# The S5 layer with a plain fp32 input projection, its tap products on one engine, and its constants and Toeplitz work in other places of the order

## The chip, the cores and the metric

The kernel runs on one core of a Trainium2 chip. Its engines are TensorE (matrix products; PE for the products and PEld for the loading of weights in the profile), VectorE (DVE), ScalarE (ACT), GpSimd (POOL) and SyncE (SP). SyncE, ScalarE and GpSimd issue transfers into DMA queues. Each engine runs its own instructions in order and waits on semaphores for the others. The metric is the device time of one execution in microseconds (us), as the median of several executions.

## The reference, cut to what matters

The kernel computes one inference step of a four-layer decoder trunk for 512 prompt tokens and 8 x 8 sampled tokens, 576 columns in all, in fp32. The change is in the token mixer of the first layer, an S5 state-space layer with 64 groups of 16 channels and 64 complex states per group:

```python
u = (x @ w_in)                                    # 1024 -> 1024
dt = jnp.exp(log_dt)[:, None]
mag = jnp.exp(lam_r * dt)
lb_r, lb_i = mag * jnp.cos(lam_i * dt), mag * jnp.sin(lam_i * dt)
den = lam_r * lam_r + lam_i * lam_i
f_r = ((lb_r - 1.0) * lam_r + lb_i * lam_i) / den
f_i = (lb_i * lam_r - (lb_r - 1.0) * lam_i) / den
bb_r, bb_i = _cmul(f_r[..., None], f_i[..., None], b_re, b_im)
bu = einsum('blgi,gpi->blgp', ug, bb)             # complex inputs of the states
h = associative_scan(h[t] = lb * h[t-1] + bu[t])  # complex states, all t
y = einsum(h_r, c_re) - einsum(h_i, c_im) + d_skip * u
g = gelu(y);  out = (g * sigmoid(g @ w_glu + b_glu)) @ w_out
```

Three more token mixers and, after each mixer, an expert channel mixer follow; the change does not touch them.

## The kernel before, in words

**The algorithm.** Time is cut into chunks of 8 steps: 64 chunks of the prompt and 8 sampled sequences, so `NC` = 72 columns. Within a chunk the layer is a Toeplitz product (tiles `T0` to `T2`, each for 16 of the 64 groups); between chunks a recurrence carries the state (tile `HS`), and a last product takes the states into the outputs. All of it stands in `s5` (from L263).

**Projection.** The input x comes in eight tiles `xraw` of 128x576. Each is split into a high and a low part of a reduced fp32 type (`x0H` by ScalarE, L130; `x0L` by VectorE, L131), and each weight block `wr` of 128x1024 into `wh` (ScalarE, L69) and `wl` (VectorE, L79). u comes in eight blocks m of 128 rows; a block takes 8 steps k, two halves of 288 columns and three products each (high by high, high by low, low by high), 384 products in all, issued in `mm` (L126). ScalarE copies a block out (L435) and writes it to the DRAM tile `du` (L436, ScalarE's queue). After every fourth block SyncE loads the four blocks back in another order into `U8` (eight transfers, L442, `U` in the rows).

**Parameters.** `params()` (L317 to L411) is a generator: the projection loop takes steps of it in between, so its small operations on VectorE stand between the splits. It works out exp, sine and cosine (128x64 tiles), the powers 0 to 8 of the step factor (`PW`, L295 to L300 through `cmul`), and the input matrix `bb`, `b2` (twelve operations of 128x512, L380 to L385). GpSimd negates halves of `c1` and `b2` (L353, L354) and makes twelve of sixteen groups of output taps `CL` (three operations of 128x576 each, `powered`, L311 to L315, called at L360). VectorE makes the eight back steps (`BL`, `tb`, six 128x512 operations each, L401), which TensorE transposes and ScalarE copies into `BT` (`turn`, L388 to L394), and then the last four groups of taps (L409).

**Order after the projection.** SyncE loads the initial state into `HS` (L450) and the skip vector `dk` (L453); GpSimd multiplies it by a diagonal into `dm` (L454) and then sets the three T tiles to zero (L458). TensorE multiplies `BT` by `U` (L488); VectorE copies the results to `HS` (L490) and ScalarE to `SS` (L491). GpSimd works out the chunk powers `AP` (L500 to L508), 24 operations in three rounds after six that set up the first power. `toeplitz(q)` (L460 to L480), for q = 0 to 3, copies `bb` on ScalarE into `BR`, multiplies it by `CL` on TensorE, copies the product to `KT`, adds `dm` on GpSimd (L476) and places the result in T with sixteen transfers, eight each from SyncE and GpSimd. `toeplitz(0)` and `toeplitz(1)` are issued ahead of the recurrence, 2 and 3 after it, followed by the products of T with `U` (L579) and their copies to `U` (L582).

**Recurrence.** `steps` (L520 to L533) makes two products and two sums on VectorE per job. The first phase goes over seven positions of the chunks (128x512 operations), the second over seven chunk blocks (128x64), the third over the seven positions again (128x448), and a last step gives the final states `HF`, with a copy (L567). `swap` (L510 to L518) puts a slice of `HS` into `H2` (`H` in the rows): two copies on ScalarE and two transfers from SyncE. One swap is issued before the recurrence; the other eight are gathered in a list and issued at L574, behind the transfers of all four `toeplitz` calls. Then the output products with `CL` and `H2` run (from L585); VectorE adds them to `U` (L596), and SyncE and GpSimd write the result to DRAM. GELU, the gate and the output projection end the layer.

`Weights` (L48) loads raw blocks ahead (three buffers), splits them, and hands them out with `next`; `next_raw` hands out a raw block.

Of the kernel before, what the change touches and what calls it, by code (L numbers as in the profile page):

```python
# [19 lines left out]
KD = 8  # L20
# [27 lines left out]
class Weights:  # L48
# [71 lines left out]
class K:  # L120
# [142 lines left out]
    def s5(self):  # L263
        tc, nc, I, O = self.tc, self.nc, self.I, self.O
        V, G, A, S = nc.vector, nc.gpsimd, nc.scalar, nc.sync
        R0, R1, R2, R3, R4, LB, L0, L1 = (ExitStack() for _ in range(8))
        p0 = self.pool(R0, "s5a")
        p1 = self.pool(R1, "s5b")
        p2 = self.pool(R2, "s5c")
# [4 lines left out]
        b1, b2, c1, c2 = (p2.tile([128, 64, 16], F32, name=k) for k in ("b1", "b2", "c1", "c2"))  # L274
        xH = p2.tile([128, KD, NT], F32R, name="x0H"); xL = p2.tile([128, KD, NT], F32R, name="x0L")
        xraw = {}

        def xload(k):
            xraw[k] = p2.tile([128, NT], F32, name="xraw", bufs=XB)
            S.dma_start(xraw[k], I["xT0"][:, k, :])  # L280
# [3 lines left out]
        for k in range(1, XB):  # L284
            xload(k)
        PW = p0.tile([128, 9, 2, 64], F32, name="PW")
# [4 lines left out]
        tg = p2.tile([128, 4, 9, 16], F32, name="tg")  # L291
# [10 lines left out]
        def powered(E, jobs, a, b, last):  # L302
# [7 lines left out]
            for o, t, pw, ab in todo:  # L310
                E.tensor_tensor(o, pw[0], ab[0], op=OP.mult)  # L311
            for o, t, pw, ab in todo:
                E.tensor_tensor(t, pw[1], ab[1], op=OP.mult)
            for o, t, pw, ab in todo:
                E.tensor_tensor(o, o, t, op=last)  # L315

        def params():  # L317
# [5 lines left out]
            for i, _ in enumerate(self.exp_(dt, ldt, p2, "e")):  # L323
# [4 lines left out]
                if i % 4 == 3:  # L328
                    yield
# [3 lines left out]
            for i, _ in enumerate(self.sincos(sn, cs, ang, p2)):  # L333
                next(ex, None)
                if i % 3 == 2:
                    yield
# [6 lines left out]
            yield  # L343
            tmp = p2.tile([128, 4, 8, 16], F32, name="BL", bufs=4).rearrange("p a b c -> p a (b c)")[:, :, :64]
            for b in (1, 2, 4):
# [4 lines left out]
                yield  # L350
# [5 lines left out]
            def taps(E, e0, t):  # L356
                e = slice(e0, e0 + 4)
                powered(E, [(CL[:, e], t, e, slice(0, 9))], c1, c2, OP.subtract)

            for e0 in range(0, 4 * NG, 4):  # L360
                taps(G, e0, tg)
# [12 lines left out]
            yield  # L374

            for h in range(2):
# [9 lines left out]
                yield  # L386

            def turn(q, BL):  # L388
                for i in range(2):
                    o = self.psB()  # L390
                    for a in range(4):
                        nc.tensor.transpose(o[:, 128 * a:128 * a + 128], BL[i][:, a].rearrange("p s j -> p (s j)"), self.ident)
                    e = 8 * q + 4 * i
                    A.activation(BT[:, e:e + 4, :].rearrange("p a b -> p (a b)"), o, AF.Copy)  # L394


            last = None
            for q in range(8):
                BL, tb = ([p2.tile([128, 4, n, 16], F32, name=k, bufs=m)[:, :, :8] for _ in range(2)] for k, n, m in (("BL", 8, 4), ("tb", 9, 2)))
                e = [slice(8 * q + 4 * i, 8 * q + 4 * i + 4) for i in range(2)]  # L400
                powered(V, [(BL[i], tb[i], e[i], slice(7, None, -1)) for i in range(2)], bb, b2, OP.subtract)  # L401
                yield
                if last:
                    turn(*last)
                last = (q, BL)
                yield
            turn(*last)
            for e0 in range(4 * NG, 64, 4):
                taps(V, e0, p2.tile([128, 4, 9, 16], F32, name="tb", bufs=2))  # L409
                yield  # L410


        par = params()
        for k in range(KD):
            self.split(xH[:, k, :], xL[:, k, :], xraw[k])
            if k + XB < KD:
                xload(k + XB)
            if k == 1:
                self.W.load(2)
            if k == 4:  # L420
                for t, n in ((b1, "b1"), (b2, "b2"), (c1, "c1"), (c2, "c2")):
                    S.dma_start(t, I[n])
            if k == 0:
                self.W.split(1)
            next(par)
        du = self.dram.tile([D, NT], F32, name="du")
        duv = du.rearrange("(g j) (s c) -> s j g c", j=16, s=8)
        for m in range(KD):
            w = self.W.next()
            o = [self.ps(), self.ps()]  # L430
            self.proj([(o[q][:, :288], slice(288 * q, 288 * q + 288)) for q in range(2)], w, xH, xL)
            self.W.ahead()
            uT = p2.tile([128, NT], F32, name="xraw", bufs=XB)
# [3 lines left out]
            for _ in range(3):  # L437
                next(par, None)
# [4 lines left out]
        for _ in par:  # L443
            pass
        R2.close()
        p2 = self.pool(R2, "s5d")
# [5 lines left out]
        dk = p2.tile([128, 32], F32, name="dk"); dm = p2.tile([128, 32, 16], F32, name="dm")  # L452
        S.dma_start(dk, I["s5_d"])  # L453
# [1164 lines left out]
```

## Time and profile before

| what | us |
|---|---|
| median of three executions | 3258.47 (3254.98 to 3260.18) |
| profiled execution, its own time | 3255.29 |
| its span, first to last instruction | 3253.5 |
| TensorE busy (PE) | 2994.6 (92%) |
| VectorE busy (DVE) | 2746.4 (84%) |
| GpSimd busy (POOL) | 1363.6 (42%) |
| ScalarE busy (ACT) | 1157.5 (36%) |

The mean granted clock of TensorE is 0.964 of full speed. Times within the profile count from the first instruction. The busy shares are averages over all four layers; the S5 layer is the first, and its first output product starts at 208.48 us. A row of the chain of waits gives start, duration and what was being waited for or done. A row of the timeline gives start, busy time, engine, line, operation, out<-in by tile names, shape, and in brackets the idle time before it with what ended it; several like operations in a row stand as one with their count (x8), and what such a row then gives is their time together. A row by stretches gives the stretch, its length, the busy us of PE, PEld, DVE, ACT and POOL with their instructions, the granted clock, the mean share of the DMA engines in use, and GB/s. "SPq" and "ACTq" are the issue of transfers by SyncE and ScalarE. The busy times of two operations of one engine that follow each other can overlap by 0.05 to 0.1 us, since an operation starts before the one ahead of it is out.

### The profile page before, as it was taken

The page shows a single profiled execution, that of the slowest core. Times are in us where ns is not written, and L with a number is a line of the kernel's source. Part 1 is how long each engine was busy: PE and PEld are TensorE (multiplying, and loading weights), DVE is VectorE, ACT ScalarE, POOL GpSimd, SP SyncE. Part 2 cuts the span into 40 slices and gives each one's busy share as a digit, 9 for nine tenths or more (in the row PEclk, how much of TensorE's full clock was granted, in tenths as well). Part 3 has the DMA queues.
Part 4 walks back from the last instruction along what each step waited for, and adds up shares of the span by engine and source line. Part 5 has one row for each costly group of instructions (what it writes and reads, how often), then busy time and mean ns, then how long its engine had stood idle before and what let it go on. Part 6 is the DMA issues. An engine that isn't in the chain of part 4 may idle for free.

```text
span 3253.5 us, 45493 instructions
## 1 busy us (share of the span) xinstructions
PE 2994.6 (92%) x16316; PEld 2561.6 (79%) x16316; DVE 2746.4 (84%) x5864; ACT 1157.5 (36%) x1704; POOL 1363.6 (42%) x994
## 2 busy tenths in 40 slices
PE   5559979899999999999998897989899999999997
PEld 4558877566899888888988797656688988888986
DVE  9846798999888888888887679899888888888888
ACT  2234232256333333333333333235533333333332
POOL 7441221444354555554430022245345555555442
PEclk8879989999999999999999998989999999999998
DMA  4364324999999999999972211689899999999995
GB/s 129 61 117 145 127 111 139 328 359 340 315 343 344 334 340 337 340 340 338 342 283 94 75 57 56 223 297 387 303 331 338 340 347 335 336 332 348 353 338 201
DMA packets 332273, 862.44 MB, mean 265 GB/s; under 512 B 56199, under 2 KB 145255, under 8 KB 329334
## 3 DMA queue, kind: packets, MB, share of 16 engines
q1 hardware_dynamic: 204830, 434.41, 38.9%
q0 software_dynamic: 112960, 405.36, 34.4%
q10 hardware_dynamic: 14256, 19.77, 1.7%
q8 instruction: 128, 2.10, 0.3%
q14 instruction: 99, 0.81, 0.1%
HBM read 791.76 MB, written 71.96 MB: 265 GB/s over the span
## 4 chain that ended last, share of the span: by engine, by line
PE 70%; DVE 19%; DMA 4%; issue 2%; ACT 2%; POOL 2%; SPq 1%; DVEq 0%; ACTq 0%; POOLq 0%
PE pa L126 41%; PE pb L126 29%; DMA grow<-in_peer_u,gidx 1%; DVE prod L1486 1%; DVE grow L1525 1%; DVE ti L1339 1%; DVE sc L1335 1%; DVE ti L1333 1%; DMA x<-SD 1%; DVE tv L1331 1%; DVE tv L1337 1%; DMA wr<-in_U 1%; DVE rs L783 1%; SPq L480 1%; DVE st L767 0%
## 5 line engine op out<-in xcount | busy, mean ns | idle before, releaser
L1520 POOL DMA_INDIRECT grow<-in_peer_u,gidx x384 | 611.2, 1592 | 516.6 <-DVE acc L1533 312.2
L1520 POOL DMA_INDIRECT grow<-in_peer_v,gidx x384 | 503.0, 1310 | 720.4 <-DVE grow L1525 561.5
L131 DVE TENSOR_TENSOR vl<-vr,vh 128x1024 fp32r<-128x1024 f32 x256 | 313.8, 1226 | 251.8 <-ACT vh L130 251.2
L126 PE MATMUL pa<-vh,wwh 128*128 128x512 f32 x1536 | 478.9, 393 | 24.9 <-ACT wwh L1217 24.7
L1533 DVE SCALAR_TENSOR_TENSOR acc<-grow,gact,acc 128x1024 f32<-128x1024 f32 x380 | 485.6, 1278 | 3.5 <-DMA grow<-in_peer_v,gidx 2.5
L1525 DVE SCALAR_TENSOR_TENSOR grow<-grow,x 128x1024 f32<-128x1024 f32 x384 | 465.2, 1217 | 23.1 <-DMA grow<-in_peer_u,gidx 21.4
L126 PE MATMUL pa<-vh,wwl 128*128 128x512 f32 x1536 | 477.7, 392 | 0.0
L126 PE MATMUL pa<-vl,wwh 128*128 128x512 f32 x1536 | 477.0, 392 | 0.0
L126 PE MATMUL pb<-xH,wl 128*128 128x384 f32 x1344 | 455.0, 339 | 0.0
L126 PE MATMUL pb<-xH,wh 128*128 128x384 f32 x1344 | 454.9, 338 | 0.0
L126 PE MATMUL pb<-xL,wh 128*128 128x384 f32 x1344 | 454.3, 338 | 0.0
L130 ACT ACTIVATE vh<-vr 128x1024 fp32r<-128x1024 f32 x256 | 271.8, 1062 | 511.3 <-PE pa L126 462.8
L126 PEld LDWEIGHTS pa<-vh,wwh 128*128 128x128 f32 x1536 | 287.2, 189 | 76.5 <-ACT wwh L1217 28.7
L126 PEld LDWEIGHTS pa<-vl,wwh 128*128 128x128 f32 x1536 | 289.3, 188 | 63.6
L126 PEld LDWEIGHTS pa<-vh,wwl 128*128 128x128 f32 x1536 | 288.8, 188 | 63.8 <-DVE wwl L1219 1.8
L79 POOL TENSOR_TENSOR wl<-wr,wh 128x1024 fp32r<-128x1024 f32 x35 | 90.3, 2580 | 405.7 <-ACT wh L69 339.7
L126 PEld LDWEIGHTS pb<-xL,wh 128*128 128x128 f32 x1344 | 253.1, 188 | 7.4
L79 DVE TENSOR_TENSOR wl<-wr,wh 128x1024 fp32r<-128x1024 f32 x193 | 237.0, 1228 | 25.3 <-ACT wh L69 25.2
L126 PEld LDWEIGHTS pb<-xH,wh 128*128 128x128 f32 x1344 | 252.3, 188 | 6.5
L126 PEld LDWEIGHTS pb<-xH,wl 128*128 128x128 f32 x1344 | 252.3, 188 | 0.0
L69 ACT ACTIVATE wh<-wr 128x1024 fp32r<-128x1024 f32 x228 | 239.4, 1050 | 12.8 <-PE pa L126 10.7
L126 PE MATMUL pb<-x,wr 128*128 128x384 f32 x704 | 238.5, 492 | 0.6 <-DMA wr<-in_U 0.6
(349 smaller groups left out, 4998.3 us busy)
## 6 DMA issues: line engine op xcount, KB each, us to landing
wr<-in_U SPq DMA_DIRECT2D x256, 512.0 KB
vr<-in_peer_v SPq DMA_DIRECT2D x256, 512.0 KB
GD<-stg SPq DMA_DIRECT2D x16, 2048.0 KB
x<-GD SPq DMA_DIRECT2D x64, 512.0 KB
SD<-g ACTq DMA_DIRECT2D x88, 192.0 KB
x<-SD SPq DMA_DIRECT2D x88, 192.0 KB
wr<-in_w_q SPq DMA_DIRECT2D x32, 512.0 KB
grow<-in_peer_u,gidx POOLq DMA_INDIRECT x384
```

Of the source, the lines that this page charges most:

```text
L69: self.k.nc.scalar.activation(h[:, :nk], self.raw[self.nh], AF.Copy)
L79: e.tensor_tensor(l[:, :nk], self.raw.pop(self.ns), h[:, :nk].bitcast(F32), op=OP.subtract)
L126: self.nc.tensor.matmul(out, lhsT, rhs, start=start, stop=stop)
L130: self.nc.scalar.activation(h, src, AF.Copy)
L131: self.nc.vector.tensor_tensor(l, src, h.bitcast(F32), op=OP.subtract)
L480: (S if par else G).dma_start(Tb[q % 3][16 * s:16 * s + 16, par::2, 16 * s:], KT[r0:r0 + 16, :, :128 - 16 * s])
L783: yield V.scalar_tensor_tensor(t, y, ve, y, op0=OP.mult, op1=OP.mult)
L1331: V.max(v[:, 0:8], s)
L1333: V.max_index(i[:, 0:8], v[:, 0:8], s)
L1520: nc.gpsimd.indirect_dma_start(out=t, out_offset=None, in_=table, in_offset=bass.IndirectOffsetOnAxis(ap=gidx[:, 128 * u + j:128 * u + j + ...
L1525: V.scalar_tensor_tensor(t, t, 1.0, self.X(3 + u), op0=OP.mult, op1=OP.mult, accum_out=act[:, 128 * u + j:128 * u + j + 1])
L1533: V.scalar_tensor_tensor(acc[:, u], t, w, acc[:, u], op0=OP.mult, op1=OP.add)
```

## The change

- **Projection.** x and the weights are not split; the products are plain fp32 ones, 128 in all. The first two blocks run together over k (`next_raws`), the others one at a time (`next_raw`). All eight `xraw` tiles have their own place; `b1`, `b2`, `c1`, `c2` are loaded between the weight blocks.
- **Parameters.** `params()` runs straight through. The negations of `b2` and `c1` go to ScalarE. The chunk powers `AP` are worked out right after `PW`: eighteen operations (`cmul`) on GpSimd, the setting up and the copies on ScalarE.
- **Taps.** All sixteen groups are made by VectorE, in pairs like the back steps, after them. A back step and half a block's projection alternate.
- **Skip and zeros.** `dk` is loaded at the start on ScalarE's queue, `dm` and the zeros of `T0` and `T1` are made by GpSimd at the start. `T2` has its own place and is set to zero after the inputs.
- **Inputs.** Both evacuations of the input products are on ScalarE; the first half of the inputs runs after three quarters of the taps.
- **Reload.** Four of the eight transfers of the second reload of `U` are issued by GpSimd.
- **Toeplitz.** `dm` is added by VectorE. `toeplitz(0)` and `toeplitz(1)` are issued before the recurrence, (2) and (3) within its first phase, the products with T (`within`) beside it.
- **Swaps.** Each is issued as soon as its slice is ready in the order. The weight split of the next projection is issued after `HF`.

The diff, cut to its core:

```diff
@@ Weights
+    def next_raws(self, n):
+        self.load(n)
+        ws = [self.raw.pop(i) for i in range(n)]
+        self.nu = self.nh = self.ns = n
+        return ws
@@ s5: loads and places
-        xH = p2.tile([128, KD, NT], F32R, name="x0H"); xL = p2.tile([128, KD, NT], F32R, name="x0L")
...
+            xraw.append(p2.tile([128, NT], F32, name=f"xraw{k}"))
...
+        xload(1)
+        xload(2)
+        self.W.load(2)
+        for k in range(3, KD):
             xload(k)
+        for t, n in ((b1, "b1"), (b2, "b2")):
+            S.dma_start(t, I[n])
+        self.W.load(3)
+        for t, n in ((c1, "c1"), (c2, "c2")):
+            S.dma_start(t, I[n])
+        dk = pt.tile([128, 32], F32, name="dk"); dm = pt.tile([128, 32, 16], F32, name="dm")
+        A.dma_start(dk, I["s5_d"])
...
+        Tb = [pt.tile([128, 16, 128], F32, name=f"T{q}") for q in range(2)]
+        G.tensor_tensor(dm, self.diag[:, None, :].to_broadcast([128, 32, 16]), dk[:, :, None].to_broadcast([128, 32, 16]), op=OP.mult)
+        for t in Tb:
+            G.memset(t, 0.0)
@@ params(): runs straight, its yields are gone
-            G.tensor_scalar(c1[im], c1[im], -1.0, None, op0=OP.mult)
-            G.tensor_scalar(b2[im], b2[im], -1.0, None, op0=OP.mult)
...
-            for e0 in range(0, 4 * NG, 4):
-                taps(G, e0, tg)
+            A.activation(b2[im], b2[im], AF.Copy, scale=-1.0)
+            A.activation(c1[im], c1[im], AF.Copy, scale=-1.0)
+
+            for h in range(2):
+                rows, e = slice(64 * h, 64 * h + 64), slice(32 * h, 32 * h + 32)
+                A.activation(AP[rows, 0, 0, 0], PW[rows, 8, 0, e], AF.Copy)
+                A.activation(AP[rows, 0, 1, 1], PW[rows, 8, 1, e], AF.Copy)
+            for b in (1, 2, 4):
+                sh = [128, b, 32]
+                cmul(G, AP[:, b:2 * b, 0, 0], AP[:, b:2 * b, 1, 1], AP[:, b - 1:b, 0, 0].to_broadcast(sh), AP[:, b - 1:b, 1, 1].to_broadcast(sh),
+                     AP[:, :b, 0, 0], AP[:, :b, 1, 1], tap[:, :b, :])
@@ back(q), turn(q, BL): the eight steps as before, now functions
+        def taps(q):
+
+            for e0 in (8 * q, 32 + 8 * q):
+                es = [slice(e0 + i, e0 + i + 4) for i in (0, 4)]
+                powered([(CL[:, e], pc.tile([128, 4, 9, 16], F32, name="tb", bufs=2), e, slice(0, 9)) for e in es], c1, c2)
@@ projection
-            self.split(xH[:, k, :], xL[:, k, :], xraw[k])
...
-            self.proj([(o[q][:, :288], slice(288 * q, 288 * q + 288)) for q in range(2)], w, xH, xL)
-            self.W.ahead()
+        def uproj(ws, os, ks):
+            for k in ks:
+                for w, o in zip(ws, os):
+                    for q in range(2):
+                        self.mm(o[q][:, :288], w[:, k, :], xraw[k][:, 288 * q:288 * q + 288], k == 0, k == KD - 1)
...
-                    S.dma_start(U8[16 * s:16 * s + 16, g, :], duv[s][:, g, :])
+                    (G if m > 3 and s % 2 else S).dma_start(U8[16 * s:16 * s + 16, g, :], duv[s][:, g, :])
...
+        first = self.W.next_raws(2)
+        o = [[self.ps(), self.ps()] for _ in range(2)]
+        uproj(first, o, range(KD))
+        for m in range(2):
+            udone(m, o[m])
+        for m in range(2, KD):
+            w, o = self.W.next_raw(), [self.ps(), self.ps()]
+            for h in range(2):
+                q = 2 * (m - 4) + h
+                if q >= 0:
+                    BL = back(q)
+                uproj([w], [o], range(4 * h, 4 * h + 4))
+                if q >= 0:
+                    turn(q, BL)
+            udone(m, o)
@@ toeplitz(q), inputs, order
-            G.tensor_tensor(KT[:, :, :16], KT[:, :, :16], dm[:, 8 * q:8 * q + 8], op=OP.add)
+            V.tensor_tensor(KT[:, :, :16], KT[:, :, :16], dm[:, 8 * q:8 * q + 8], op=OP.add)
...
-            V.tensor_copy(HS[:, 9:, :, gp:gp + 2], ov[:, 8:])
+                A.activation(HS[:, 9:, :, gp:gp + 2], ov[:, 8:], AF.Copy)
...
+        for q in range(3):
+            taps(q)
+        inputs(range(0, 16, 2))
+        toeplitz(0)
+        taps(3)
+        toeplitz(1)
+        A.activation(AP[:, :, 0, 1], AP[:, :, 0, 0], AF.Copy)
+        A.activation(AP[:, :, 1, 0], AP[:, :, 1, 1], AF.Copy, scale=-1.0)
+        inputs(range(16, 32, 2))
...
+        G.memset(Tb[2], 0.0)
@@ recurrence
         for q in range(1, 8):
             steps([(H[:, :, q], H[:, :, q - 1], H[:, :, q], AP[:, 0, 0], AP[:, 0, 1])])
+            if q == 2:
+                toeplitz(2)
+                within(0)
+            if q == 5:
+                toeplitz(3)
+                within(1)
         for b in range(1, 8):
             steps([(H[:, b:b + 1, 7], H[:, b - 1:b, 7], H[:, b:b + 1, 7], AP[:, 7, 0], AP[:, 7, 1])])
-        swaps = [lambda: swap(slice(16, 73, 8))]
+        within(2)
+        within(3)
+        swap(slice(0, 9))
+        swap(slice(16, 73, 8))
         for q in range(0, 7, 2):
...
-                swaps.append(lambda i=i: swap(slice(9 + i, 73, 8)))
+                swap(slice(9 + i, 73, 8))
...
+        self.W.split(self.W.nu + 2)
```

## Rows read from the trace of the kernel before

**Rows 1.** Page, chain that ended last: share of span by engine.

```profile
PE 70%; DVE 19%; DMA 4%; issue 2%; ACT 2%; POOL 2%; SPq 1%; DVEq 0%; ACTq 0%; POOLq 0%
```

**Rows 2.** Busy us by engine (x instructions), granted clock, DMA share, GB/s, by stretch.

```profile
40.00:90.00 50.00, 19.50 (x108) 17.86 (x108) 50.00 (x30) 4.76 (x9) 49.22 (x30) 0.67 0.34 57
90.00:121.00 31.00, 27.55 (x198) 26.81 (x200) 27.73 (x42) 11.10 (x21) 0.25 (x1) 0.90 0.25 80
```

**Rows 3.** Chain that ended last, 100 to 230: start, us, what.

```profile
121.31 13.80 issue
...
136.20 5.24 POOL T L458 x3
...
143.53 0.74 POOL AP L295
...
173.15 11.23 POOL KT L476
...
206.04 2.31 DMA H<-HS
```

**Rows 4.** Timeline of VectorE (start, us, operation), 142 to 188: recurrence.

```profile
142.35 0.69 DVE L528 TENSOR_TENSOR w<-AP,HS 128x512 f32<-128x512 f32 x1 [1.78 <-POOL AP L500]
...
163.60 0.23 DVE L528 TENSOR_TENSOR w<-AP,HS 128x64 f32<-128x64 f32 x1
...
169.52 0.62 DVE L528 TENSOR_TENSOR w<-AP,HS 128x448 f32<-128x448 f32 x1
...
184.78 0.68 DVE L528 TENSOR_TENSOR w<-AP,HS 128x512 f32<-128x512 f32 x1
...
187.30 0.19 DVE L567 COPY HF<-HS 128x64 f32<-128x64 f32 x1
```

**Rows 5.** Timeline of VectorE, 38 to 119 us: the big products and taps.

```profile
38.93 1.72 DVE L380 TENSOR_TENSOR bb<-sn,b 128x512 f32<-128x512 f32 x1
...
61.41 3.50 DVE L311 TENSOR_TENSOR BL<-PW,bb 128x512 f32<-128x512 f32 x2
...
94.26 1.28 DVE L313 TENSOR_TENSOR tb<-PW,b 128x512 f32<-128x512 f32 x2
95.47 1.28 DVE L315 TENSOR_TENSOR BL<-BL,tb 128x512 f32<-128x512 f32 x2
...
118.03 0.75 DVE L311 TENSOR_TENSOR CL<-PW,c 128x576 f32<-128x576 f32 x1
```

**Rows 6.** Timeline of ScalarE and VectorE, 3 to 26: parameters.

```profile
4.00 0.68 ACT L130 ACTIVATE x0H<-xraw 128x576 fp32r<-128x576 f32 x1 [0.56 <-DMA xraw<-in_xT]
...
7.64 0.22 DVE L321 TENSOR_TENSOR den<-lr 128x64 f32<-128x64 f32 x1
...
24.47 0.22 DVE L295 TENSOR_TENSOR PW<-PW 128x64 f32<-128x64 f32 x1
```

**Rows 7.** TensorE: timeline 510 to 545 us, and chain 100 to 230 us.

```profile
515.52 29.83 PE L126 MATMUL pa<-x,wr 128*128 128x384 f32 x92
...
111.66 6.28 PE pa L126 x47
```

**Rows 8.** Timeline of SyncE, ScalarE and TensorE, 55 to 140: reloads of U.

```profile
62.11 21.82 SPq L442 DMA_DIRECT2D U<-du  x8
...
118.71 0.33 ACTq L436 DMA_DIRECT2D du<-xraw  x1
...
120.82 7.23 SPq L442 DMA_DIRECT2D U<-du  x8
...
134.53 5.58 PE L126 MATMUL pa<-U,BT 128*64 128x72 f32 x128 [5.08 <-DMA U<-du]
```

**Rows 9.** Timeline of GpSimd and ScalarE, 184 to 198: T copies, U copies.

```profile
184.67 4.17 POOL L480 DMA_DIRECT2D T<-KT  x8 [0.30 <-POOL KT L476]
188.84 0.46 POOL L476 TENSOR_TENSOR KT<-KT,dm 128x128 f32<-128x128 f32 x1
...
196.46 0.41 ACT L582 ACTIVATE U<-pa 128x288 f32<-128x288 f32 x1 [0.55 <-PE pa L126]
```

More of the change, by code (lines that the diff above doesn't have):

```diff
@@ L265, in s5 @@
         V, G, A, S = nc.vector, nc.gpsimd, nc.scalar, nc.sync
-        R0, R1, R2, R3, R4, LB, L0, L1 = (ExitStack() for _ in range(8))
+        R0, R1, R2, R4, RT, RH, LB, LC, L0, L1 = (ExitStack() for _ in range(10))
         p0 = self.pool(R0, "s5a")
         p1 = self.pool(R1, "s5b")
-        p2 = self.pool(R2, "s5c")
+        pc = LC.enter_context(tc.tile_pool(name="s5c", bufs=1, reuse_waits="tile"))
+        pt = self.pool(RT, "s5e")
+        p2 = self.pool(R2, "s5p")
         small = lambda n: p2.tile([128, 64], F32, name=n)
@@ L397, in params @@
[L397 to L414, printed above, removed]
-            self.split(xH[:, k, :], xL[:, k, :], xraw[k])
[L416 to L425, printed above, removed]
+        def back(q):
+            BL, tb = ([p.tile([128, 4, n, 16], F32, name=k, bufs=m)[:, :, :8] for _ in range(2)] for p, k, n, m in ((p2, "BL", 8, 4), (pc, "tb", 9, 2)))
+            e = [slice(8 * q + 4 * i, 8 * q + 4 * i + 4) for i in range(2)]
+            powered([(BL[i], tb[i], e[i], slice(7, None, -1)) for i in range(2)], bb, b2)
+            return BL
@@ L426, in s5 @@
+        params()
         du = self.dram.tile([D, NT], F32, name="du")
         duv = du.rearrange("(g j) (s c) -> s j g c", j=16, s=8)
-        for m in range(KD):
-            w = self.W.next()
-            o = [self.ps(), self.ps()]
-            self.proj([(o[q][:, :288], slice(288 * q, 288 * q + 288)) for q in range(2)], w, xH, xL)
-            self.W.ahead()
-            uT = p2.tile([128, NT], F32, name="xraw", bufs=XB)
+        def uproj(ws, os, ks):
[3 more added lines that the diff above has]
+                        self.mm(o[q][:, :288], w[:, k, :], xraw[k][:, 288 * q:288 * q + 288], k == 0, k == KD - 1)
@@ L434, in s5, with udone @@
+        def udone(m, o):
+            uT = p2.tile([128, NT], F32, name="uT", bufs=2)
             for q in range(2):
@@ L451, in s5 @@
         G.memset(HS[:, 8], 0.0)
[L452 to L458 removed]
         def toeplitz(q):
[L463 removed]
+            BR = p2.tile([128, 2, 8, 4, 16], F32, name="BR")
             for par in range(2):
@@ L492, in s5 @@
-        LB.close()
-        H2 = self.pool(R4, "s5h").tile([128, 73, 2, 32], F32, name="H2")
-        AP = p2.tile([128, 8, 2, 2, 32], F32, name="AP")
-        tap = p2.tile([128, 4, 32], F32, name="tap")
-        for h in range(2):
-            rows, e = slice(64 * h, 64 * h + 64), slice(32 * h, 32 * h + 32)
-            G.tensor_copy(AP[rows, 0, 0], PW[rows, 8, 0:1, e].to_broadcast([64, 2, 32]))
-            G.tensor_scalar(AP[rows, 0, 1, 0], PW[rows, 8, 1, e], -1.0, None, op0=OP.mult)
-            G.tensor_copy(AP[rows, 0, 1, 1], PW[rows, 8, 1, e])
@@ new lines, in within @@
+        def within(q):
+            for g4 in range(0, 16, 4):
+                o = self.ps()
+                for a in range(4):
+                    for h in range(2):
+                        rows = slice(64 * h, 64 * h + 64)
+                        self.mm(o[rows, NC * a:NC * a + NC], Tb[q % 3][:, g4 + a, rows], U8[:, 16 * q + g4 + a, :], True, True)
+                g = 16 * q + g4
+                A.activation(U8[:, g:g + 4, :].rearrange("p a c -> p (a c)"), o[:, :4 * NC], AF.Copy)
+        for q in range(3):
+            taps(q)
```

111 lines of the change are left out of this document (36 added, 75 removed).

## The prediction

> **What bounds the kernel now.** The whole execution is bound by TensorE: its products are most of the chain that ended last [rows 1]. That share is an average over stages, and the change edits only the first, from the start to the first output product of the state-space layer at 208.5 us. So I read the stretches of that stage next [rows 2]: VectorE is busy all of 40 to 90 us, TensorE two fifths of them; from 90 to 121 both are busy nine tenths. The chain of waits says what leads: first VectorE, then the rest of the projection on TensorE, and from 121 a chain that does not run on VectorE [rows 3]: a 13.8 us wait for the second reload of U, which also covers the wait for the skip vector; three memsets on GpSimd (5.24 us); 24 small GpSimd operations of the chunk powers, one after the other, from 143.53 (0.74 the first) to 161.6; the Toeplitz copies; a GpSimd addition that took 11.23 us; copies issued by SyncE; and the last copy into H, from 206.04 to 208.35. VectorE had finished its own last work at 187.5 [rows 4], 21 us before.
>
> The second reading is what VectorE's operations cost. Beside GpSimd's taps a pair of 128x512 products takes 3.50 us, some 1.71 each from start to start; from 92 us on, with GpSimd idle, 1.28 (94.26 to 95.47: 0.60 each), and a 128x576 tap is busy 0.75, about 0.675 from start to start as the same 0.07 overlaps [rows 5]. Each of VectorE's big operations in 40:90 thus lost 1.1 us to GpSimd's taps.
>
> By a rule of the Trainium skill ("SBUF — State Buffer", section "SBUF: two separate sides") VectorE and GpSimd share a port pair as an exclusive lock, and the loser waits a whole instruction; the trace agrees (1.71 beside, 0.60 alone).
>
> **The change, part by part.** I follow VectorE, since after the change it holds nearly all the serial work, and look for each step at what could be later than it.
>
> *Small operations.* VectorE now starts its parameters when they land; the first tile landed by 4.0 us, so 4.4. Before, den to the powers took 16.8 us (7.64 to 24.47); without seven splits of x (0.67 each from start to start), a weight split (1.14) and 0.9 us of GpSimd's interference that is 10.1. From there to the first 128x512 product (38.93) were 14.5 us; without a split (1.1) and what GpSimd stretched in seven operations (7.2 together) 6.2 [rows 5, 6]. The new GpSimd product dm gets 1 us. End: 21.7.
>
> *The big products.* 12 for bb at 0.60: 7.3. 48 for the eight back steps at 0.60: 29.0. All 48 taps at 0.675: 32.4, of which 24.3 before the first Toeplitz addition. The two additions, moved from GpSimd, 0.3 each.
>
> *Chunk powers on GpSimd,* now beside bb. Eighteen of the 24 operations stay, the other six go to ScalarE. Before, they ran beside 28 recurrence operations, which took 21.25 us (142.35 to 163.60) instead of the 17.6 of the undisturbed rate [rows 3, 4]: 3.6 us for 24. I take 4 for 18, as VectorE now has fewer gaps; the ends are 0 (all in gaps) and 13 (18 at 0.74, the whole chain). Two of the memsets (1.75 each) now lie beside two-input VectorE operations, which no row shows: 0 to 3.5; I take 0, as they kept an even 1.75 beside VectorE's copies [rows 3].
>
> Running sum: 21.7 + 7.3 + 4 + 29.0 = 62.0; with 24.3 + 0.3 + 8.1 + 0.3 the recurrence starts at 95.0.
>
> *Recurrence.* Seven steps at 2.52 per four operations, 17.6, plus 1.1 for two Toeplitz additions and a memset; the second phase 5.9 (163.60 to 169.52); the third 15.3 (169.52 to 184.78) [rows 4]: 134.9. The last swap is now issued at once, and needs what it needs now: 2.31 from its second issue to the landing [rows 3], and 0.9 for the first issue and the hand-over. First output product: **138.1** instead of 208.5, that is 70.4 earlier.
>
> *What must stay hidden for this.* (1) TensorE's projection: 128 plain products in place of 384. No row has one of 288 columns; the nearest is 92 plain products of 384 in 29.83 us, 0.324 each, by columns 0.243 for 288, against 0.134 for one of the three products replaced (47 in 6.28) [rows 7]. The bounds are 0.134 and 0.324; I take 0.243. A half block is eight products, 1.94, and eight transposes, put at 0.134 each too, 1.07: 3.0 us beside a back step of 3.6. Cover: 0.6 a step. The granted clock was 0.67 in 40:90 [rows 2]; at the lower level a half takes 6.0, but then TensorE is busy throughout, and rows 2 show the clock back at 0.90 when it was nearly so. Four buffers absorb two steps: cost 0 to 3, I take 0. (2) U's second reload: last block out at 64.7, written by 66.8 (2.1 as in 118.71 to 120.82 [rows 8]), 13.7 until the last load is used [rows 8], 80.5; ScalarE's two copies for each of eight groups 6.6 at most (0.41 each [rows 9], an estimate from a larger copy): 87.1, with 7.9 us of cover before 95.0. Four of these loads go to GpSimd's queue, behind the chunk powers there. (3) Toeplitz copies: sixteen issues each, eight on GpSimd in 4.17 [rows 9], eight on SyncE in 7.2 at most, its rate for U [rows 8]; the last begun by 110 and landed by 120, under the third phase of the recurrence. SyncE's waits stand in program order: behind the wait for the last copies stand only swaps that are due later. (4) Weight loads behind U's first reload on SyncE: due at 47, free to go at 32.
>
> *After the stage* the kernel is unchanged, and its TensorE-bound rest shifts whole: I know of no later transfer that starts at a fixed time. The two weight splits that are moved (128x1024 each, some 2.4 us together by 0.60 per 512 columns) end at about 140, before the first output product's result is due.
>
> **Sum.** The profiled execution took 3255.3 us (span 3253.5 and 1.8 around it), the median of three is 3258.5. 3255.3 - 70.4 = 3184.9 in the profile's own terms, 3188.1 against the median; I predict 3188.
>
> **Rivals.** *GpSimd starved.* The 11.23 us addition [rows 3] took 0.46 the next time [rows 9]: VectorE ran paired, gapless operations and GpSimd got in only at a gap. If the chunk powers meet this during bb, back steps and taps, which are paired likewise, they end only when VectorE itself stops for them at 95: 13 us of powers, 2.1 for four U loads, 6.9 for their landing (half of 13.7), 6.6 for the copies: 28.6 later, less the 4 of interference, 3188 + 24.6 = **3213**. Against it: in 40 to 90 us both engines took turns through the same paired operations. 20 in 100.
>
> *A reload stuck on SyncE.* Of U's first reload seven loads went within 4 us, the eighth 17 us later, after a later du write [rows 8]. The same at the second: 80.5 + 17 + 6.6 = 104.1 instead of 95: **3197**. 10 in 100.
>
> *The plain product is dearer than its row.* If one cost four of the single products (0.536), a half block would take 4.29 + 1.07 = 5.4 and TensorE would pace the eight back steps, 1.8 each beyond 3.6; the taps would end some 14 later: **3202**. The row (0.324 at 384 columns, against 0.18 for a single product of that width by the same ratio) speaks clearly against it. 3 in 100. The Trainium skill ("FP8 and Floating Point Precision", section "TensorE Precision Notes") has true fp32 as four passes, which is this case; the row disagrees, with less than two.
>
> *Slower.* If VectorE's operations do not shorten when GpSimd leaves, 108 big operations at 1.70 instead of 0.64 add 115 us: the products start at 249, **3299**. It decides from 1.29 us per operation (70.4/108 more than 0.64). The 0.60 of the stretch after 92 us speaks against it. 2 in 100. That the change does nothing (within 0.2%) gets 1.
>
> **How the numbers follow.** My forecast has 60 in 100. Its own ends: all small costs at their lower end (start, no interference) gives 130, 3180; memsets, powers at half their upper end and a TensorE lag give 151, 3201. The range of 8 in 10 takes in the stuck reload and the starved GpSimd: 3179 to 3214. The other 4 in 100 are stalls that I have not named. 0.2%, 6.5 us, is about what a measurement here can tell from no change; all cases but two lie far beyond it: faster 0.97, same 0.01, slower 0.02.
>
> **What would show it.** Right: 128x512 products at 0.6 us from 23 us on; the recurrence starting near 95 and the first output product near 138, with VectorE the chain between; the projection's products 0.24 apart. Wrong: a VectorE gap before the recurrence (U, or the powers on GpSimd); GpSimd operations of over 2 us in 22 to 95; back steps over 4 us apart (TensorE); or a stage that ends at 138 and a total that falls by much less, which would mean that the rest does not shift whole.

## The result, and the profile after

The changed kernel took 3198.91 us (median of four executions, 3194.87 to 3200.56) against 3256.72 (3253.99 to 3260.18) for the kernel before, measured again beside it: a ratio of 0.982 with a 95% interval of 0.9803 to 0.9837, 57.8 us less. The forecast was 3188, the range 3179 to 3214. The profiled execution took 3198.16 us, its span is 3195.9 and its mean granted clock 0.972.

The stage that the change edits ends 59.4 us earlier: the first output product starts at 149.05 instead of 208.48. The forecast had 138.1. So all of the gain is in the stage, and it is 11.0 us smaller than forecast. What follows the stage is as much earlier to within 2.1 us: 59.6 at 500 us, 58.6 at 1200, 57.3 at the end. These last differences are near to what kernels with the same stage show among themselves (a second profile of the changed kernel has the first output product at 149.40, and a kernel whose stage ends at 149.13 runs 1.2 us ahead of it at the end), so they are left.

The chain that ended last, on the page of after, share of the span by engine, which answers to [rows 1]:

```profile
PE 73%; DVE 18%; DMA 5%; issue 2%; ACT 1%; POOL 1%; SPq 1%; DVEq 0%; POOLq 0%; ACTq 0%
```

The stretches by engine, 40 to 90 and 5 to 80 us of after (columns as in [rows 2]):

```profile
40.00:90.00 50.00, 46.25 (x360) 37.70 (x358) 42.55 (x68) 18.37 (x48) 2.92 (x5) 1.00 0.62 109
5.00:80.00 75.00, 73.15 (x326) 57.32 (x328) 65.55 (x166) 15.82 (x36) 15.87 (x21) 1.00 0.59 162
```

In 40 to 90 us TensorE went from 19.50 us busy to 46.25, and VectorE from 50.00 to 42.55: the two have changed places, and GpSimd, busy 49.22 there before, is almost idle. From 5 to 80 us TensorE is busy 73.15 of 75. It is the engine that hardly waits (0.69 and 0.64 us, for weights), though it has fewer products to make. The clock is no cause of it: granted in full, 1.00, that is 2.4 GHz.

Now TensorE and VectorE during the back steps, from 45 to 60 us of after. First the timeline of TensorE, then that of VectorE (columns as in [rows 4]):

```profile
45.51 4.05 PE L133 MATMUL pa<-xraw,wr 128*128 128x288 f32 x16
49.39 1.04 PE L417 MATMUL pb<-ident,BL 128*128 128x128 f32 x8
50.26 4.05 PE L133 MATMUL pa<-xraw,wr 128*128 128x288 f32 x16
54.15 1.04 PE L417 MATMUL pb<-ident,BL 128*128 128x128 f32 x8
```

```profile
50.03 1.29 DVE L335 TENSOR_TENSOR BL<-PW,bb 128x512 f32<-128x512 f32 x2 [1.05 <-PE pb L417]
51.24 1.29 DVE L337 TENSOR_TENSOR tb<-PW,b 128x512 f32<-128x512 f32 x2
52.44 1.29 DVE L339 TENSOR_TENSOR BL<-BL,tb 128x512 f32<-128x512 f32 x2
54.78 1.29 DVE L335 TENSOR_TENSOR BL<-PW,bb 128x512 f32<-128x512 f32 x2 [1.05 <-PE pb L417]
```

VectorE's operations are what was forecast, a pair of 128x512 in 1.29 us and 3.6 for the six, and the taps (not shown) go at 1.34 a pair. But a step starts every 4.75 us (50.03 to 54.78) and waits 1.05 for TensorE's transposes. TensorE has no gap: half a block of the projection from 45.51 to 49.39, 3.88 us, and eight transposes to 50.26. The half block has sixteen instructions, where the forecast counted eight products. The groups by line and shape for TensorE, before and after, over the whole projection (columns: line, engine, operation, tiles, shape, count, busy us and mean ns, idle time before):

```profile
L126 PE MATMUL pa<-x0H,wh 128*128 128x288 f32 x128 | 31.2, 328 | 6.5 <-ACT wh L69 6.5
```

```profile
L133 PE MATMUL pa<-xraw,wr 128*128 128x288 f32 x256 | 67.0, 421 | 6.8 <-DMA wr<-in_w_in 6.8
```

The code makes 128 plain products (8 blocks, 8 steps k, 2 halves); the trace has 256 instructions. A plain product is two instructions of 3.88/16 = 0.2425 us, 0.485 in all. The reduced type is one instruction per product (128 of high by high for 128 in the code). At this pace the projection is 256 x 0.2425 = 62.1 us of work for TensorE (the row has 67.0 busy, as its first 144 instructions, from 5.52 to 44.63 us, were slower), where the three single products before are 384 x 0.134 = 51.5 at theirs [rows 7]: the change makes TensorE's work longer, not shorter, by 10.6 us.

The end of the stage went as forecast. The recurrence on VectorE starts at 106.05 (95.0 forecast), with no wait ahead of it; the timeline of VectorE and the chain of after (chain: start, us, what):

```profile
105.85 0.31 DVE L487 TENSOR_TENSOR KT<-KT,dm 128x128 f32<-128x128 f32 x1
106.05 0.71 DVE L552 TENSOR_TENSOR w<-AP,HS 128x512 f32<-128x512 f32 x1
```

```profile
146.54 2.32 DMA H<-HS
148.85 0.20 issue
149.05 4.50 PE pa L133 x62
```

The recurrence took 39.7 us where 39.9 was forecast (first phase 19.2 for 18.7, second 5.4 for 5.9, third 15.1 for 15.3), and from its end at 145.79 to the first product are 3.3 for 3.2; the last swap's transfer takes the 2.3 us that it took before [rows 3].

### The profile page after: what moved, and what is told of

Same layout as the page of the kernel before. It is cut to its first block, busy times and chain, and to the rows that moved or that the text cites. A ratio compares the mean times of both kernels' runs of the same rounds, so it can differ in the third digit from the quotient of the medians.

```text
span 3195.9 us, 45180 instructions
## 1 busy us (share of the span) xinstructions
PE 2993.5 (94%) x16188; PEld 2549.7 (80%) x16188; DVE 2713.2 (85%) x5872; ACT 1150.6 (36%) x1712; POOL 1270.6 (40%) x944
## 4 chain that ended last, share of the span: by engine, by line
PE 73%; DVE 18%; DMA 5%; issue 2%; ACT 1%; POOL 1%; SPq 1%; DVEq 0%; POOLq 0%; ACTq 0%
PE pa L133 42%; PE pb L133 30%; DMA grow<-in_peer_u,gidx 1%; DVE prod L1502 1%; DVE ti L1355 1%; DVE sc L1351 1%; DVE ti L1349 1%; DVE grow L1541 1%; DMA x<-SD 1%; DVE tv L1347 1%; DVE tv L1353 1%; DVE rs L799 1%; POOL grow L1536 1%; DVE prod L1520 0%; DVE st L783 0%
## 5 line engine op out<-in xcount | busy, mean ns | idle before, releaser
L79 DVE TENSOR_TENSOR wl<-wr,wh 128x1024 fp32r<-128x1024 f32 x185 | 225.5, 1219 | 23.7 <-ACT wh L69 23.6
L69 ACT ACTIVATE wh<-wr 128x1024 fp32r<-128x1024 f32 x220 | 230.9, 1050 | 11.3 <-PE pa L133 11.3
```

The costliest lines, as they stand in the source:

```text
L69: self.k.nc.scalar.activation(h[:, :nk], self.raw[self.nh], AF.Copy)
L79: e.tensor_tensor(l[:, :nk], self.raw.pop(self.ns), h[:, :nk].bitcast(F32), op=OP.subtract)
```

## The experiments

All were timed beside the kernel before; the table gives what each stage time came to. "Last projection product" is the start of its last instruction, "H" is the start of the first output product, "HS" the end of the last copy of the inputs into `HS`, which the recurrence needs. The totals of different rows differ by up to 4 us for the same stage, so the readings go by the stage times, and the totals are their control.

| kernel | last projection product | HS | recurrence | H | median us | ratio to before (95%) |
|---|---|---|---|---|---|---|
| changed kernel | 78.58 | 104.16 | 106.05 | 149.05 | 3198.91 | 0.982 (0.9803 to 0.9837) |
| the same, again | 78.96 | 105.36 | 106.45 | 149.40 | 3198.46 | 0.9825 (0.9811 to 0.9838) |
| half of the products | 65.75 | 89.70 | 97.90 | 140.87 | 3189.46 | 0.9789 (0.9773 to 0.9806) |
| taps in between | 78.60 | 106.12 | 106.16 | 149.13 | 3194.93 | 0.9803 (0.9787 to 0.9819) |
| zeros on ScalarE | 78.12 | 103.70 | 105.61 | 148.57 | 3197.96 | 0.9818 (0.9802 to 0.9835) |
| taps on GpSimd | 105.38 | 131.11 | 131.14 | 174.11 | 3222.57 | 0.9891 (0.9875 to 0.9908) |
| Toeplitz and swaps late | 79.23 | 104.91 | 106.71 | 173.91 | 3224.02 | 0.99 (0.9875 to 0.9925) |
| reload by two blocks | 87.48 | 106.42 | 114.97 | 158.02 | 3209.76 | 0.9857 (0.9833 to 0.988) |
| the same, and taps in between | 87.22 | 106.32 | 107.37 | 150.42 | 3200.22 | 0.9826 (0.9803 to 0.9848) |
| all second loads on SyncE | 78.16 | 103.51 | 105.65 | 148.73 | 3199.19 | 0.9819 (0.9796 to 0.9843) |
| both edits, loads on GpSimd | 77.94 | 95.40 | 97.99 | 141.03 | 3188.48 | 0.9799 (0.9786 to 0.9812) |
| and zeros on ScalarE | 77.62 | 95.33 | 97.67 | 140.70 | 3188.91 | 0.9799 (0.9785 to 0.9812) |

### Does TensorE pace the back steps? Half of the products left out

```diff
-                uproj([w], [o], range(4 * h, 4 * h + 4))
+                uproj([w], [o], (0, 2) if h == 0 else (5, 7))
```

> The changed kernel, with half of the projection's products left out in blocks 2 to 7 (four of the eight steps k), so that TensorE's part of a half block falls from 4.75 us (16 instructions of 0.2425 and eight transposes) to 2.8. Theory, TensorE paces the back steps: they go at VectorE's own 3.6 us each instead of 4.7, the recurrence starts at 97.4 instead of 106.05 and the first output product at 140.4 instead of 149.05; the total falls by some 8 us. Rival, the back steps wait for buffers or ScalarE's copies, whatever the products take: still 4.75 apart, 149.

Measured: H at 140.87 for 140.4 of the theory, the total 9.5 us less. The back steps follow each other at VectorE's own rate (timeline of VectorE, this kernel):

```profile
43.72 1.28 DVE L335 TENSOR_TENSOR BL<-PW,bb 128x512 f32<-128x512 f32 x2
47.33 1.28 DVE L335 TENSOR_TENSOR BL<-PW,bb 128x512 f32<-128x512 f32 x2
50.95 1.28 DVE L335 TENSOR_TENSOR BL<-PW,bb 128x512 f32<-128x512 f32 x2
```

The step's first pairs stand at 43.72, 47.33 and 50.95, 3.6 us apart, with no wait in brackets. With the same buffers and the same copies on ScalarE, nothing but the length of the projection has changed, so the rival (buffers, copies) falls.

### Is that all of it? Two pairs of taps moved in between

```diff
+                if q in (2, 5):
+                    pair(0 if q == 2 else 32)
                 if q >= 0:
                     BL = back(q)
```

(`pair(e0)` is half of `taps`; the two pairs drop out of `taps(0)`.)

> The changed kernel with two of the eight pairs of tap operations (4.0 us each) moved in between the back steps, ahead of steps 2 and 5, where VectorE waits for TensorE; TensorE's order is as it was. Theory, two late paths: VectorE gets 8.0 us back and reaches the end of its taps at some 98, but the second reload of U (loads issued from 84, used at 97.7, inputs in HS at 104.2) is paced by TensorE too and then sets the start of the recurrence, 104.3 instead of 106.05: first output product at 147.3, total 2 us less. Rival, VectorE's waits are the whole loss: 141.0, total 8 us less.

Measured: H at 149.13, no gain in the stage. VectorE did get its time back, and lost it in one wait further on (timeline of VectorE, this kernel):

```profile
97.93 0.28 DVE L494 TENSOR_TENSOR KT<-KT,dm 128x128 f32<-128x128 f32 x1
106.16 0.69 DVE L559 TENSOR_TENSOR w<-AP,HS 128x512 f32<-128x512 f32 x1 [7.94 <-ACT HS L510]
```

It was done at 98.2 and waited 7.94 us for the last copy into `HS`. That is the theory's second path, the projection's last block, its write to DRAM, the reload of U, the inputs. The theory had it end at 104.3; it ended at 106.12. Some 1.1 us of that are a later start of the inputs (98.78), the rest a slower run of them (6.92 us for 128 instructions, 6.04 in the changed kernel, 4.22 for the first half, when TensorE had not been idle before). The granted clock goes with it: 0.60 here (98 to 106 us), 0.68 in the changed kernel (97 to 104), both between the two levels of 1.2 and 2.4 GHz and after 4.42 and 5.77 us without work, and 1.00 for the first half (79 to 84). The total fell by 4.0 us with an unchanged stage; the ranges overlap, and no part of it is claimed.

### Do the zeros matter? ScalarE writes them

```diff
-            G.memset(t, 0.0)
+            A.activation(t, self.ident[:, None, :].to_broadcast([128, 16, 128]), AF.Copy, scale=0.0)
```

> The changed kernel with the zeros of T0 and T1 written by ScalarE at the start instead of GpSimd. Both theories have the operation that took 4.11 us on VectorE at 8 us back at 0.2 and the first big product 3.5 earlier, near 23.5. Theory, TensorE paces the back steps and the reload: the 3.5 us are lost again in the waits of the back steps; first output product at 148.5 to 149.1, total unchanged. Rival, VectorE sets the stage: 145.5, total 3.5 us less.

Measured: the first big product at 23.72 instead of 27.04, and H at 148.57. So the two zeros cost VectorE 3.3 us, and almost nothing of that reaches the end of the stage (0.5 us, where two profiles of the changed kernel differ by 0.35): the third back step now waits 4.36 us for TensorE where it waited 1.28, and starts at the same time (timeline of VectorE, this kernel, then the changed kernel):

```profile
45.04 1.29 DVE L335 TENSOR_TENSOR BL<-PW,bb 128x512 f32<-128x512 f32 x2 [4.36 <-PE pb L417]
```

```profile
45.27 1.29 DVE L335 TENSOR_TENSOR BL<-PW,bb 128x512 f32<-128x512 f32 x2 [1.28 <-PE pb L417]
```

### What did the taps' move bring? Twelve groups back on GpSimd

```diff
+            for e0 in range(0, 48, 4):
+                powered([(CL[:, e0:e0 + 4], tg, slice(e0, e0 + 4), slice(0, 9))], c1, c2, G)
...
             for e0 in (8 * q, 32 + 8 * q):
+                if e0 < 48:
+                    continue
```

> The changed kernel with twelve of the sixteen tap groups back on GpSimd, behind the chunk powers, as before the change; all else stays. Theory, the two engines slow each other to 1.71 us per operation: GpSimd's 36 operations end near 100, VectorE has done 36 of its 48 back operations by then, 12 more at 0.60 and 12 taps at 0.675 and 0.6 for the additions: recurrence at some 115.5, first output product at 158.5, 9.5 later than with all taps on VectorE. Rival, VectorE's operations keep 0.60 beside GpSimd: the reload of U sets the start at 104.3, 147.3.

Measured: H at 174.11, 25.1 us later than with the taps on VectorE, against 9.5 expected. The mechanism is there: pairs of VectorE and single operations of GpSimd take turns, at 1.7 us each (timelines of VectorE and GpSimd, this kernel):

```profile
46.78 3.51 DVE L338 TENSOR_TENSOR tb<-PW,b 128x512 f32<-128x512 f32 x2
50.22 3.51 DVE L340 TENSOR_TENSOR BL<-BL,tb 128x512 f32<-128x512 f32 x2
```

```profile
46.39 1.73 POOL L340 TENSOR_TENSOR CL<-CL,tg 128x576 f32<-128x576 f32 x1
48.08 1.67 POOL L336 TENSOR_TENSOR CL<-PW,c 128x576 f32<-128x576 f32 x1
```

The rest of the price is on the second path. In the changed order half a block stands behind the transposes of the step before, so slow back steps hold the projection up too (timeline of TensorE, then of VectorE):

```profile
62.19 0.63 PE L420 MATMUL pb<-ident,BL 128*128 128x128 f32 x4 [2.46 <-DVE BL L340]
64.01 1.09 PE L420 MATMUL pb<-ident,BL 128*128 128x128 f32 x4 [1.18 <-DVE BL L340]
```

```profile
115.84 0.29 DVE L492 TENSOR_TENSOR KT<-KT,dm 128x128 f32<-128x128 f32 x1 [7.08 <-ACT KT L490]
...
131.14 0.69 DVE L557 TENSOR_TENSOR w<-AP,HS 128x512 f32<-128x512 f32 x1 [10.80 <-ACT HS L508]
```

TensorE waits 2.46 and 1.18 us for `BL` in a step; the last projection product is 26.8 us later, at 105.38, and `HS` at 131.11. VectorE was done at 120.3, of which 7.08 are a wait for `KT`, whose products stand on TensorE behind the late projection; then it waited 10.80 more. Less the 7.08 it would have been done at 113.3, near the 115.5 expected, which was VectorE's path alone.

### What did the order behind the recurrence cost? Toeplitz work and swaps late again

The steps with `toeplitz(2)`, `toeplitz(3)` and the four `within` go behind `HF`, with eight swaps in a list that is issued ahead of the last `within`:

```diff
-            if q == 2:
-                toeplitz(2)
-                within(0)
...
+        for q in range(4):
+            if q < 2:
+                toeplitz(q + 2)
+            if q == 3:
+                for sl in swaps:
+                    swap(sl)
+            within(q)
```

> The changed kernel with the Toeplitz work of q = 2 and 3, all products with T and eight of the nine swaps behind the recurrence, in the order they had before the change. Theory, SyncE's queue is the path: the addition of dm at 148.4, sixteen T copies of 0.64 each to some 159, then sixteen swap copies of 0.62 to 169 and 2.3 for the landing: first output product at 171.5 instead of 149.05, total 22 us more. Rival, the copies go while something else is late anyway: less than 5 us more.

Measured: H at 173.91 (171.5 expected), 24.9 us later; the total is 25 us more. SyncE's queue from the end of the recurrence on (timeline of SyncE, this kernel):

```profile
149.46 11.70 SPq L491 DMA_DIRECT2D T<-KT  x16
161.21 10.84 SPq L542 DMA_DIRECT2D H<-HS  x16
```

Sixteen T copies and then sixteen swap copies stand between the recurrence and the output products, as they did before the change.

### Can the reload be started earlier? By two blocks, alone and with the taps in between

```diff
-            if m % 4 == 3:
-                g = slice(8 * (m - 3), 8 * m + 8)
+            if m % 2 == 1:
+                g = slice(8 * (m - 1), 8 * m + 8)
```

> The changed kernel with U loaded back after every second block instead of every fourth (transfers of half the size, twice as many). Theory, VectorE reaches the recurrence last in the changed kernel: the second half of the inputs starts some 6 us earlier, near 92 instead of 97.7, and the recurrence still starts at 106.0, first output product at 149.0, total unchanged. Rival, the reload is what the recurrence waits for: some 6 us less.

> Both edits together: two pairs of taps in between the back steps, and U loaded back after every second block. Theory, two late paths that must both be shortened: recurrence at 98.0 to 98.5, first output product at 141.0 to 141.5, total 8 us less than the changed kernel, though the taps alone were to give 2 and the reload alone nothing. Rival, one of the two alone sets the stage: no more than the better one alone.

Measured: both theories missed; of the rivals the second's outcome came (no more than the better one alone, 149.13), but not for its reason. H at 158.02 and 150.42, no better than the changed kernel, and the first 9 us worse. The last projection product is at 87.5. The cause stands in SyncE's queue and in what TensorE waits for (timelines of SyncE and TensorE, the reload alone):

```profile
32.34 3.87 SPq L446 DMA_DIRECT2D U<-du  x8
37.31 1.30 SPq L60 DMA_DIRECT2D wr<-in_w_in  x3
```

```profile
24.70 8.89 PE L133 MATMUL pa<-xraw,wr 128*128 128x288 f32 x36
41.02 13.57 PE L133 MATMUL pa<-xraw,wr 128*128 128x288 f32 x48 [7.43 <-DMA wr<-in_w_in]
```

SyncE waited until 32.3 for the first two blocks to be in DRAM; the weights of the next block stood behind these loads, were issued at 37.3, and TensorE stood still for 7.43 us. That is the rival "a reload stuck on SyncE" of the prediction, turned round: not a load of U behind a write, but the weights behind a load of U.

### Are four loads on GpSimd's queue worth anything? All eight on SyncE

```diff
-                    (G if m > 3 and s % 2 else S).dma_start(U8[16 * s:16 * s + 16, g, :], duv[s][:, g, :])
+                    S.dma_start(U8[16 * s:16 * s + 16, g, :], duv[s][:, g, :])
```

> The changed kernel with all eight transfers of the second reload of U issued by SyncE, as before the change. Issue then takes 7.2 us instead of 2.8. Theory, the landing is set by the transfers themselves, as both kernels have 13.7 us from the first issue to the first use: no change, first output product at 149.0. Rival, the last issue sets the landing: inputs some 4.5 us later, recurrence at 108.6, 151.6, total 2.6 us more.

Measured: H at 148.73, total 3199.19: no difference. The first use of the second half is 13.5 us after the first issue (83.07 to 96.61) with eight issues in 5.68 us, and 13.8 (83.94 to 97.69) with four on each queue. This part of the change did nothing.

### Both late paths shortened: taps in between, reload by two blocks, all loads on GpSimd

```diff
-                    (G if m > 3 and s % 2 else S).dma_start(U8[16 * s:16 * s + 16, g, :], duv[s][:, g, :])
+                    G.dma_start(U8[16 * s:16 * s + 16, g, :], duv[s][:, g, :])
```

(with the two edits above: two pairs of taps in between, and U loaded back after every second block)

> As the run before with both edits (taps in between, U loaded back after every second block), but all loads of U are issued by GpSimd, so that no weight load stands behind them in SyncE's queue. Theory, the reload edit failed because block 3's weights came 7.4 us late behind U's loads: the projection's last product is back at 78.6 or earlier instead of 87; the last eight loads are issued from 84 to 89 (0.6 each) and landed by some 93.5, the inputs are in HS by 100, the recurrence starts there and the first output product at 143; total 6 us less than the changed kernel. Rival, smaller loads or GpSimd's queue are slow in themselves: HS not before 106, 149 or later.

> The run with GpSimd's loads, and in addition the zeros of T0 and T1 on ScalarE. Theory, TensorE and the reload set the start of the recurrence: VectorE's 3.4 us are lost again, first output product at 142.5 to 143. Rival, VectorE sets it: 139.5.

> The changed kernel once more, beside the two others on the same chip: first output product within 0.7 us of 149.05, as e3 and e9, which changed nothing on its path, were.

(In the last of these, e3 is the run with the zeros on ScalarE and e9 the one with all second loads on SyncE.)

Measured: H at 141.03, and the total 3188.48 against 3198.46 for the changed kernel beside it, 10.0 us less (medians of five executions; the ratios to the kernel before are 0.9799, 0.9786 to 0.9812, and 0.9825, 0.9811 to 0.9838). The changed kernel's own H was 149.40, within the 0.7 us expected. No weights are late any more (the last projection product is at 77.94), GpSimd issues the last eight loads in 4.44 us, and the inputs are in `HS` at 95.40, 2.6 us before VectorE is done (timelines of GpSimd and VectorE, this kernel):

```profile
83.33 4.44 POOL L451 DMA_DIRECT2D U<-du  x8 [14.54 <-DMA du<-uT]
```

```profile
97.79 0.28 DVE L494 TENSOR_TENSOR KT<-KT,dm 128x128 f32<-128x128 f32 x1
97.99 0.68 DVE L559 TENSOR_TENSOR w<-AP,HS 128x512 f32<-128x512 f32 x1
```

I had expected 143, with the reload still last; it was quicker than that, and VectorE is last. With the zeros on ScalarE as well H is at 140.70: VectorE starts its back steps 1.5 us earlier and waits for TensorE instead. The theory named the outcome (no gain from the zeros) but not the time (142.5 to 143), since the reload was no longer last; the rival's 139.5 is not reached either. This version is faster than both kernels of the case.

## Why the prediction was right, and by how much it was not

**The direction and the range held, the point was 10.9 us low.** What was to bring the gain did: GpSimd's taps gone, VectorE's operations go at their own rate, and the late Toeplitz work and swaps are off the path. Undone alone, the taps' move costs 25.1 us of the stage and the order behind the recurrence 24.9; if the two add, which no run shows, they are 50 of the 59.4. The move of the chunk powers, zeros and skip to the start was not undone alone, so its share stays open. Nor was the plain projection: it takes splits off VectorE and ScalarE and gives TensorE more to do, and whether that pays on balance no run shows.

That the total fell within the range is in part luck. The range was drawn to take in the stuck reload and the starved GpSimd, and neither came; for TensorE, which made most of the miss, the forecast had 0 to 3 us. One of its own signs of being wrong did show: back steps over 4 us apart, paced by TensorE.

**The step that failed is cover (1), TensorE's projection.** It put a plain product of 288 columns at 0.243 us, from 92 rows in 29.83 us [rows 7]. The size is right (0.2425), but it is that of an instruction: the row counts instructions, and a plain product has two. A half block takes 4.75 us instead of 3.0, the eight back steps 37.65 instead of 29.0. By the run with half of the products this costs 8.2 of the 11.0 us (H at 140.87 without it). The case was among the rivals ("the plain product is dearer than its row", 3202, measured 3198.9), with 0.536 for a product where 0.485 was measured, and got 3 in 100. It got so little since the count in the row was never held against the code. The rows had the means for it: the 128 instructions of [rows 8] are half of the inputs, for which the code makes 64 products.

The Trainium skill ("FP8 and Floating Point Precision", section "TensorE Precision Notes") has a true fp32 product as four passes. By a single product's 0.134 us that is an estimate of 0.536; the trace has 0.485, 3.6 of them. The prediction held the row against this rule, and the rule was nearer.

**The second reload had 1.9 us of cover, not 7.9** (1.1 in the second profile). The write of the last block was issued at 81.19 instead of 64.7, so `HS` was ready at 104.16 instead of 87.1, just ahead of the recurrence at 106.05 (timelines of ScalarE, SyncE, TensorE and ScalarE, changed kernel):

```profile
81.19 0.33 ACTq L442 DMA_DIRECT2D du<-uT  x1
...
83.94 1.92 SPq L446 DMA_DIRECT2D U<-du  x4
...
97.69 6.04 PE L133 MATMUL pa<-U,BT 128*64 128x72 f32 x128 [5.77 <-issue]
...
103.76 0.40 ACT L503 ACTIVATE HS<-pa 128x256 f32<-128x256 f32 x1
```

The terms behind that write came out as forecast to within 0.7 us each (2.75 for 2.1, 13.75 for 13.7, 6.47 for 6.6); it is the late projection that they start from. With the taps in between this path becomes the last. The taps alone gave 0, the reload alone -9, as it made weights late, and both without that wait 8.0 to 8.4. The reload without the weights' wait and without the taps was not run; that it would give nothing is argued from VectorE's own 106.05.

**Three smaller terms were wrong, and were covered.** The first big product came at 27.04 instead of 21.7. The parameters landed at 5.6 and 6.5 us, not by 4.4; the zeros held VectorE for 3.6 us (3.3 by the run with the zeros on ScalarE), where I had taken 0 of a bound of 3.5 and had only two-input operations beside them, while the one that was held has one input; the chunk powers took 2.4 (1.6 in `bb`, 0.8 in the first back step) where I had taken 4. With the projection halved they show as the other 2.8 us (140.87 against 138.1). In the changed kernel they lie under TensorE's pace: the run with the zeros on ScalarE takes 3.3 us off the start and gains 0.5 at the end.

**The rivals.** GpSimd was not starved: its eighteen operations ran beside `bb` at 0.9 us or less each and were done at 38.0. The reload was not stuck; a weight load was, behind a `du` write, until 56.9 us, and cost TensorE 0.64 us. The operations did shorten. And the stage's gain came through to the end, to 2.1 us.

## What to carry to other kernels

Before an instruction's mean time is put into a sum, hold its count in the trace against the count of calls in the code; a product that is cheap per instruction can be two instructions. When work is taken off the engine that sets the pace, work out the next engine's whole stretch from its first to its last instruction, not its share per step: here TensorE had 69 us of work at full clock (62.1 of products, 7.0 of transposes) in a stretch of 74, from 5.5 to 79.8 us. And where two paths end within 2 us of each other, an edit to one of them can gain 2 us at most, which here did not show; move both before judging either, and look at what stands behind each new wait in an in-order queue.

## What the runs showed of the hardware

A plain fp32 product of 288 columns was issued as two instructions of 0.2425 us at full clock, where one of the reduced type took 0.134.

A zeroing memset on GpSimd stopped some operations of VectorE for its whole length and left others alone. Timelines of VectorE and GpSimd at the start, in the changed kernel and in the kernel with GpSimd's loads:

```profile
7.98 4.11 DVE L235 TENSOR_SCALAR ei<-e 128x64 int32<-128x64 f32 x1
8.53 3.56 DVE L236 SCALAR_TENSOR_TENSOR e<-e,e 128x64 f32<-128x64 f32 x1
...
8.50 3.54 POOL L315 MEMSET T<- 128x2048 f32 x2
```

```profile
8.37 3.68 POOL L315 MEMSET T<- 128x2048 f32 x2
8.40 0.21 DVE L236 SCALAR_TENSOR_TENSOR e<-e,e 128x64 f32<-128x64 f32 x1
...
8.53 1.73 DVE L237 TENSOR_SCALAR ei<-ei 128x64 int32<-128x64 int32 x1
...
10.34 1.78 DVE L240 SCALAR_TENSOR_TENSOR e<-e,e 128x64 f32<-128x64 f32 x7
```

In the first an operation with one SBUF input (L235) that began ahead of the two memsets ended only behind them, 4.11 us later; the next one was queued behind it. In the second the two-input operation (8.40) ran in 0.21 us beside the first memset, the one-input operation behind it (8.53) ended when that memset did, and seven two-input ones ran unhindered beside the second. In all eight other traces with these two memsets, L235 ended behind the second of them, as in the first picture. Before the change three memsets stood beside half of the sixteen copies out of PSUM into `HS` and slowed none: each of the sixteen took 0.41 to 0.43 us.

The Trainium skill ("SBUF — State Buffer", section "SBUF: two separate sides") agrees in kind: it has two-input operations of VectorE contend only with GpSimd operations that read SBUF, and those in a two-port mode with any. That the one-input operations here ran in such a mode no run shows.
